# Latent rows turned by VectorE and DMA instead of TensorE in a two-layer hybrid trunk

## The chip, the core and the metric

The kernel runs on one core of a Trainium2 chip. The metric is the device time of one execution in microseconds; the median of three runs of the kernel before is 1133.07 us (1133.02 to 1134.05).

## The reference

A backbone of two layers with 256 latent tokens and 256 context tokens, width 2048, in float32. Each layer makes one wide input projection (5120 columns), three branches (a gated position-mixing MLP, windowed attention that also reads the context, Fourier mixing), gates them, concatenates them and projects back. Only the latents are returned, after the second layer.

```python
h = rmsnorm(x, g_pre[l]) * (1.0 + scale[:, None]) + shift[:, None]
h_c = rmsnorm(ctx, g_pre[l]) * (1.0 + scale_c) + shift_c
proj = h @ w_in[l]
...
y = mixer_branches(proj, latent_attn, g_sgu[l], w_sgu[l], b_sgu[l], w_fourier[l], b_fourier[l])
y = rmsnorm(y @ w_out[l], g_post[l])
x_new = x + gate[:, None] * y
```

The last line is where the change lies: in the second layer it adds x1, the latents that the first layer returned, to the gated and normalised projection.

## The kernel before

**Layout.** Nearly everything is held transposed: features on the 128 partitions, tokens along the free dimension. The tile `yo[k]` (k from 0 to 15) holds features 128k to 128k+127 of both streams, latents in columns 0 to 255 (`LAT`), context in 256 to 511 (`CTX`). After the first layer `yo[k][:, LAT]` holds x1, transposed. The output, however, has rows of tokens: the last projection (phase out1, function `finish`) takes 128 tokens at a time as the stationary operand and so makes its result with tokens on the partitions. Before the sum, x1 has to be turned to rows of tokens, in eight tiles of 128 tokens by 512 features: `x1[j, t]` for four groups of features j and two blocks of tokens t.

**Matmuls.** Float32 precision is had from two parts, a high and a low one: each weight tile of 128x1024 is loaded into one of three `raw` buffers (L433), cast to `whi` by ScalarE (ACT, L456), and the rest `wlo` is made by VectorE (DVE, L458). Products take three matmuls (`mm3`, L488 to L490) or two (`mm2`, L604 and L605). The function `fetch` keeps the split three tiles ahead of TensorE (PE); there are four buffers for each part.

**Order.** PE's instructions run in the order in which the program is written. Those of DVE, ACT, SP (SyncE, which issues the loads) and POOL are put in order by a scheduler, before the run; each engine then runs its list in that order, and an instruction that waits holds up all those behind it. Side work is written as generators and handed to a small planner (`Later`): each has a due time in a model clock that advances with the main matmuls (`later.tick`), runs to its next `yield` when it is due, and gives the delay to its next step there. `later.flush()` runs what is left.

**Layer 1 in order of time.** First units av and au (742 to 774 us), then fourteen units of one or two streams: au, cx (Fourier), ag and cg (gates), to 864 us; a flush; then k (to 886) and v (to 909) of both streams, eight q units with the attention heads as side work, eight bg units, and the last projection from 1029.5 us on. Side work between 778 and 868 us is the second half of branch A (`ps_mix`), the Fourier steps (`ps_f`, `ps_z`), and `boundary_ctx`: the context's new residual (`yo[k][:, CTX]`, DVE at L1279, then a DMA by POOL at L1280 that adds the old context to it), the sum of its squares (ACT L1284, DVE L1286, PE `ps_rs` L526) and its normalised form for k and v (L566, L570, L575).

**The gate of layer 1** (`mod_gate1`, L287 to L291) is a product of a vector with w_mod on DVE: 32 loads of 512 KB into two buffers `mraw`, two instructions of DVE for each, spread by `pace` over the phases k1, v1, q1, bg1 and out1 at low priority. Its four results lie in `ctrh`, `ctrl`, `nstrh` and `nstrl`; `gate1` finishes them (L302 to L309).

**The turn before** is the generator `turn` in `finish` (L1138 to L1149): four transposes by PE into a PSUM bank and one ACT copy to SBUF for each `x1[j, t]`, one every `YT` = 3.0 of the model clock. The tiles it writes are vv, mg, mgl, kt0 and kt1, which attention used before; `vv` is also the buffer of the Fourier weights early in the layer, and of the values of attention from the v units on. `close` reads the x1 tiles at the end.

Of the kernel before, what the change touches and what calls it, by code (L numbers as in the profile page):

```python
# [7 lines left out]
F32 = mybir.dt.float32  # L8
# [5 lines left out]
P = 128  # L14
D = 2048
KT = D // P
S = 256
# [49 lines left out]
def trunk_kernel(ctx: ExitStack, tc: tile.TileContext, xT, xhalf, cT, wss, wsl, wmod, win, wout0, wout1, const, vec, rows,  # L67
                 wmat, bs, sink, out):
    nc = tc.nc
    V, A, G, PE, DMA = nc.vector, nc.scalar, nc.gpsimd, nc.tensor, nc.sync  # L70

    pool = ctx.enter_context(tc.tile_pool(name="sb", bufs=1))
    psum = ctx.enter_context(tc.tile_pool(name="ps", bufs=1, space=bass.MemoryType.PSUM))
    W2K = 7
    cnt = [0]

    def sb(shape, dt, tag, bufs=1):
        cnt[0] += 1
        return pool.tile(shape, dt, tag=tag, bufs=bufs, name=f"{tag}_{cnt[0]}")

    def w2k(shape, dt=F32):
        return sb(shape, dt, "w2k", W2K)

# [4 lines left out]
    def ms_ps(name="ms"):  # L88
        cnt[0] += 1
        return psum.tile([P, 512], F32, tag="ms", bufs=2, name=f"ps_{name}_{cnt[0]}")  # L90


    yo = [sb([P, T], F32, f"yo{k}") for k in range(KT)]
# [42 lines left out]
    ident = identr.bitcast(F32)  # L136
# [195 lines left out]
    BYDVE = {10: 7, 15: 7}  # L332
    RING = "ctrl nstrl kt1 ws bsb hh11 hl11 ctrl yo8 nstrl kt1 ws bsb yo9 yo10 yo11".split()
    LOWC = 60
    YT = 3.0
    GATES = {2: 0, 14: 1}, {14: 2}, {12: 3}, {}
    YG = 6.5
    WARM = 4
# [38 lines left out]
    later = Later()  # L377
# [109 lines left out]
    def mm3(ps, st, mv, start, stop):  # L487
        PE.matmul(ps, st[0], mv[0], start=start, stop=False)  # L488
        PE.matmul(ps, st[0], mv[1], start=False, stop=False)  # L489
        PE.matmul(ps, st[1], mv[0], start=False, stop=stop)  # L490
# [13 lines left out]
    def split_into(hi, lo, src):  # L504
        A.copy(hi, src)  # L505
        V.tensor_tensor(out=lo, in0=src, in1=hi.bitcast(F32), op=ALU.subtract)  # L506
        return hi, lo
# [79 lines left out]
    FULL, LAT, CTX = slice(0, T), slice(0, S), slice(S, T)  # L587
    PASS = 0.648 / T

    def tunit(n, sl=None):  # L590

        sl = slice(0, n) if sl is None else sl
        ps = mm_ps("t")
        for k in range(KT):
            if k % 8 == 0:
                w = W.next()
            c = slice((k % 8) * P, (k % 8 + 1) * P)
            mm3(ps[:, sl], part(w, c), (hh[k][:, sl], hl[k][:, sl]), k == 0, k == KT - 1)
            later.tick(PASS * n)
        return ps  # L600
# [13 lines left out]
    def tunit1(streams):  # L614

        pss = [mm_ps("t") for _ in streams]
        for k in range(KT):
            if k % 8 == 0:
                w = W.next()
            for s, ps in zip(streams, pss):  # L620
                mm2(ps, part(w, slice((k % 8) * P, (k % 8 + 1) * P)), (hh, hl)[s][k], k)
                later.tick(PASS * S)
        return [joined(ps) for ps in pss]
# [12 lines left out]
    def layer(l):  # L636
        last = l == 1
# [241 lines left out]
        def fourier_mats():  # L879
            for j in range(2):  # L880
                ps = ms_ps("mg")
                mm3(ps, csp[j], wfp, True, True)
                split_into(mg[0][:, :, j], mg[1][:, :, j], ps.rearrange("p (g d) -> p g d", d=P))
            yield 0.0
# [47 lines left out]
        kt, vv = [], None  # L932
# [80 lines left out]
            later.add(turn_mask(), 7.0)  # L1013
        later.add(branch_a())
        later.add(fourier_mats(), 3.0)
        later.tick(0.0)
        state["phase"] = f"au{l}"
        for h in range(len(au), 4):
            ps = tunit1([0])[0] if last else tunit(n)
# [3 lines left out]
        for g in range(4):  # L1023
            ps = tunit1([0])[0] if last else tunit(n)
# [3 lines left out]
        for h in range(4):  # L1028
            ps = tunit1([0])[0] if last else tunit(n)
            gate(h, ps)  # L1030
        state["phase"] = f"cg{l}"
        for g in range(4):
            ps = tunit1([0])[0] if last else tunit(n)
# [11 lines left out]
        vv = sb([P, 1024], F32R, "vv"), sb([P, 1024], F32R, "mg")  # L1045
# [12 lines left out]
        for h in range(8):  # L1058
            ps = tunit1([0])[0] if last else tunit(n)
# [3 lines left out]
        for h in range(8):  # L1063
            ps = tunit1([0])[0] if last else tunit(n)
# [35 lines left out]
    def out_proj():  # L1100
# [30 lines left out]
        later.flush()  # L1131
        return acc

    def finish():

        x1 = {}

        def turn():  # L1138

            for j, tag in enumerate(("vv", "mg", "mgl", "kt0 kt1")):  # L1140
                tag = tag.split()
                tl = [sb([P, 2 // len(tag), 512], F32, t) for t in tag]
                for t in range(2):
                    x1[j, t] = tl[0][:, t] if len(tl) == 1 else tl[t][:, 0]
                    ps = ms_ps("x1")
                    for i in range(4):
                        PE.transpose(ps[:, i * P:(i + 1) * P], yo[4 * j + i][:, t * P:(t + 1) * P], ident)
                    A.copy(x1[j, t], ps)
                    yield YT  # L1149

        later.add(turn(), YT)
        state["phase"] = "out1"
        state["ones"] = sb([P, P], F32R, "join", 2)
# [161 lines left out]
    with tc.manual_schedule(engines={EN.PE}):  # L1315
# [12 lines left out]
        for k in range(KT):  # L1328
            q = w2k([P, T])
# [14 lines left out]
        ps = ms_ps("rs")  # L1344
# [16 lines left out]
        make_h(0, 0, rb0, [0, 1], e)  # L1361
        list(e)
        layer(0)
        state["acc"] = out_proj()
        layer(1)
        finish()


# [75 lines left out]
```

## Time and profile before

| | us |
|---|---|
| median of three runs | 1133.07 |
| profiled execution | 1132.31 |
| its span | 1130.5 |
| PE busy | 1122.0 |
| DVE busy | 927.6 |
| ACT busy | 528.5 |
| POOL busy | 33.7 |

The span is the time from the first to the last instruction of the profiled execution. Busy times of PE overlap with its weight loads (PEld). A row of the profile gives an engine, the line of the kernel, the operation, and the tile written and the tiles read; in a row of the timeline the first two numbers are the start and the length in us, and the bracket at its end is the idle time of that engine just before, with what ended it. "SPq" is SP's queue, where a DMA is issued; the DMA share is the mean busy share of the 16 DMA engines.

### The profile page before, as it was taken

Reading aid. Unit: us, or ns where it says so; the run is one execution under the profiler, and the core shown is the slowest. Engines: PE = TensorE matmul, PEld = TensorE weight load, DVE = VectorE, ACT = ScalarE, POOL = GpSimd, SP = SyncE. Lnnn points to the kernel's source line nnn. Section 1 sums busy time; section 2 is a strip of 40 time slices with the busy share of each in tenths; the row PEclk is TensorE's granted clock in tenths of the full one; section 3 lists DMA queues with packets and bytes.
Section 4 is the critical chain, followed back from the end, with each engine's and each line's share of the span. In section 5 each row is a group of like instructions: output and inputs, shape, how many; then the busy total and the mean of one; then the engine's idle time right before and its main releaser. Section 6 shows DMA issues by size and latency. Waiting matters only on the chain.

```text
span 1130.5 us, 16656 instructions
## 1 busy us (share of the span) xinstructions
PE 1122.0 (99%) x6117; PEld 921.5 (82%) x6117; DVE 927.6 (82%) x1649; ACT 528.5 (47%) x991; POOL 33.7 (3%) x41
## 2 busy tenths in 40 slices
PE   8999999999999999999999999999999999999998
PEld 3666788888888888888888888988888888888886
DVE  1578799989888788898999988397889789878883
ACT  5322433322235666642533334256665369857551
POOL 0000000000000000000000000030500000000000
PEclk9999999999999999999999999999999999999999
DMA  9999656566656344356556665276956686556972
GB/s 350 403 402 400 243 181 202 170 206 192 215 175 188 107 140 131 122 180 211 186 170 223 221 212 179 94 170 213 226 168 197 214 295 195 158 170 198 315 251 75
DMA packets 75250, 235.85 MB, mean 209 GB/s; under 512 B 8736, under 2 KB 13216, under 8 KB 75168
## 3 DMA queue, kind: packets, MB, share of 16 engines
q1 hardware_dynamic: 70992, 230.85, 61.4%
q0 software_dynamic: 4032, 3.67, 2.2%
q8 instruction: 48, 0.79, 0.3%
q14 instruction: 34, 0.28, 0.1%
q10 hardware_dynamic: 144, 0.26, 0.1%
HBM read 232.65 MB, written 2.10 MB: 208 GB/s over the span
## 4 chain that ended last, share of the span: by engine, by line
PE 96%; DVE 1%; ACT 1%; DMA 0%; issue 0%; SPq 0%; POOLq 0%; DVEq 0%; ACTq 0%
PE ps_t L488 15%; PE ps_t L490 15%; PE ps_t L489 15%; PE ps_t L604 10%; PE ps_t L605 5%; PE ps_v L1053 3%; PE ps_y L488 3%; PE ps_y L490 3%; PE ps_y L489 3%; PE ps_mod L181 2%; PE ps_av L488 2%; PE ps_av L489 2%; PE ps_av L490 2%; PE ps_tp L995 1%; PE ps_v L1054 1%; PE ps_au L488 1%
## 5 line engine op out<-in xcount | busy, mean ns | idle before, releaser
L456 ACT CAST whi<-raw 128x1024 fp32r<-128x1024 f32 (+1 forms) x209 | 216.4, 1037 | 320.6 <-PE ps_t L489 221.9
L488 PE MATMUL ps_t<-hh,whi 128*128 128x512 f32 (+1 forms) x752 | 290.6, 386 | 0.0
L490 PE MATMUL ps_t<-hh,wlo 128*128 128x512 f32 (+1 forms) x752 | 289.7, 385 | 0.0
L489 PE MATMUL ps_t<-hl,whi 128*128 128x512 f32 (+1 forms) x752 | 289.6, 385 | 0.0
L458 DVE TENSOR_TENSOR wlo<-raw,whi 128x1024 fp32r<-128x1024 f32 (+1 forms) x209 | 250.9, 1203 | 45.8 <-ACT whi L456 40.0
L253 DVE SCALAR_TENSOR_TENSOR macc<-mraw,cs,macc 128x512 f32<-128x512 f32 x360 | 250.0, 745 | 11.5 <-DMA mraw<-in_wmod_dram 11.2
L604 PE MATMUL ps_t<-hh,whi 128*128 128x512 f32 x512 | 184.9, 399 | 0.0
L490 PEld LDWEIGHTS ps_t<-hh,wlo 128*128 128x128 f32 x752 | 141.3, 188 | 28.5
L488 PEld LDWEIGHTS ps_t<-hh,whi 128*128 128x128 f32 x752 | 141.3, 188 | 26.9
L489 PEld LDWEIGHTS ps_t<-hl,whi 128*128 128x128 f32 x752 | 141.3, 188 | 26.4
L605 PE MATMUL ps_t<-hh,wlo 128*128 128x256 f32 x512 | 143.4, 280 | 0.0
L604 PEld LDWEIGHTS ps_t<-hh,whi 128*128 128x128 f32 x512 | 96.2, 188 | 21.5
L605 PEld LDWEIGHTS ps_t<-hh,wlo 128*128 128x128 f32 x512 | 96.6, 189 | 0.4
L570 ACT ACTIVATE hh<-w2k,sh 128x256 fp32r<-128x256 f32 x48 | 22.1, 503 | 72.7 <-DVE w2k L566 72.7
L488 PE MATMUL ps_y<-whi,hh 128*128 128x512 f32 x104 | 41.3, 397 | 0.0
L490 PE MATMUL ps_y<-whi,hh 128*128 128x512 f32 x104 | 40.6, 390 | 0.0
L489 PE MATMUL ps_y<-wlo,hh 128*128 128x512 f32 x104 | 40.5, 389 | 0.0
L488 PE MATMUL ps_av<-whi,hh 128*128 128x512 f32 x94 | 39.0, 415 | 0.6 <-ACT hh L570 0.6
L489 PE MATMUL ps_av<-wlo,hh 128*128 128x512 f32 x94 | 37.1, 395 | 0.0
L505 ACT CAST w2k<-ps_tp 128x512 fp32r<-128x512 f32 x40 | 23.4, 586 | 20.3 <-PE ps_scc L489 8.6
L518 POOL TENSOR_TENSOR rs_b<-rs_a,mhalf 128x2 f32<-128x2 f32 (+1 forms) x6 | 6.6, 1096 | 776.8 <-DVE mx L1245 584.8
L506 DVE TENSOR_TENSOR w2k<-ps_tp,w2k 128x512 fp32r<-128x512 f32 x40 | 27.4, 684 | 1.3 <-ACT w2k L505 0.5
(458 smaller groups left out, 1777.0 us busy)
## 6 DMA issues: line engine op xcount, KB each, us to landing
raw<-in_win_dram SPq DMA_DIRECT2D x160, 512.0 KB, 4.1
mraw<-in_wmod_dram SPq DMA_DIRECT2D x128, 512.0 KB, 4.2
raw<-in_wout_dram SPq DMA_DIRECT2D x60, 512.0 KB, 4.4
mraw<-in_wsl_dram SPq DMA_DIRECT2D x14, 512.0 KB, 7.2
yo<-in_xT_dram SPq DMA_DIRECT2D x16, 256.0 KB, 5.3
yo<-in_wsl_dram SPq DMA_DIRECT2D x16, 256.0 KB, 7.2
macc<-in_wsl_dram SPq DMA_DIRECT2D x7, 512.0 KB, 7.7
vv<-in_wsl_dram SPq DMA_DIRECT2D x7, 512.0 KB, 8.4
```

Of the source, the lines that this page charges most:

```text
L181: PE.matmul(self.ps[32 * kk:32 * kk + 32, 0:self.N], cpad[:, kg * 4 + kk], self.w[kg * 4 + kk], start=kg == 0, stop=kg == 3, tile_position ...
L253: V.scalar_tensor_tensor(out=acc[:, s], in0=w[:, kk % 2], scalar=c, in1=acc[:, s], op0=ALU.mult, op1=ALU.add)
L456: A.copy(ph, rc)
L458: self.last = V.tensor_tensor(out=pl, in0=rc, in1=ph.bitcast(F32), op=ALU.subtract)
L488: PE.matmul(ps, st[0], mv[0], start=start, stop=False)
L489: PE.matmul(ps, st[0], mv[1], start=False, stop=False)
L490: PE.matmul(ps, st[1], mv[0], start=False, stop=stop)
L505: A.copy(hi, src)
L506: V.tensor_tensor(out=lo, in0=src, in1=hi.bitcast(F32), op=ALU.subtract)
L604: PE.matmul(ps, w[0], h, start=k == 0, stop=False)
L605: PE.matmul(ps[:, 0:S], w[1], h[:, 0:S], start=False, stop=k == KT - 1)
L1053: PE.matmul(vps[t], hi, wk, start=k == 0, stop=False)
```

## The change

x1 is now turned during layer 1 by a new generator, `x1_rows`, which is started in the second layer beside branch A and the Fourier weights, with a delay of 7.0 and a step every `YS` = 6.0 of the model clock. It takes the buffer `vv` for four pieces of 128x256. Step k turns `yo[k][:, LAT]` with VectorE's transpose, which works in squares of 32x32: within each square rows and columns are exchanged, and the squares stay where they are. Two steps later four DMAs, one for each band of 32 partitions, put the squares in their places in a scratch tile in DRAM, `x1d[g]`, of 256 tokens by 512 features; each moves 32 x 8 runs of 32 floats. That is 16 transposes and 64 DMAs on SP's queue. In `finish`, `turn` loads each `x1[j, t]` (128 tokens by 512 features, 256 KB) from the scratch with one DMA, in place of the four PE transposes and the ACT copy. `YT` is 6.0 instead of 3.0.

```diff
+    dram = ctx.enter_context(tc.tile_pool(name="dram", bufs=1, space=bass.MemoryType.DRAM))
...
-    YT = 3.0
+    YT, YS = 6.0, 6.0
...
         later.add(fourier_mats(), 3.0)
+        if last:
+            later.add(x1_rows(), 7.0)
...
+    x1d = {}
+
+    def x1_rows():
+        v = sb([P, 4, S], F32, "vv")
+        ts = [v[:, i] for i in range(4)]
+        for k in range(KT + 2):
+            if k >= 2:
+                g, i = divmod(k - 2, 4)
+                if i == 0:
+                    x1d[g] = dram.tile([S, 512], F32, tag=f"x1_{g}", name=f"x1_{g}")
+                for q in range(4):
+                    f = i * P + 32 * q
+                    DMA.dma_start(x1d[g][:, f:f + 32].rearrange("(b t) f -> t b f", t=32),
+                                  ts[i][32 * q:32 * q + 32].rearrange("p (b f) -> p b f", f=32))
+            if k < KT:
+                V.transpose(ts[k % 4], yo[k][:, LAT])
+                yield YS
...
-                    ps = ms_ps("x1")
-                    for i in range(4):
-                        PE.transpose(ps[:, i * P:(i + 1) * P], yo[4 * j + i][:, t * P:(t + 1) * P], ident)
-                    A.copy(x1[j, t], ps)
+                    DMA.dma_start(x1[j, t], x1d[j][t * P:(t + 1) * P])
                     yield YT
```

## The prediction

> **What bounds the kernel now.** I read the page first (busy shares, then the chain that ended last), and after it the busy time by stretch for layer 1 and the last projection.
>
> ```profile
> span 1130.5 us, 16656 instructions
> PE 1122.0 (99%) x6117; PEld 921.5 (82%) x6117; DVE 927.6 (82%) x1649; ACT 528.5 (47%) x991; POOL 33.7 (3%) x41
> PE 96%; DVE 1%; ACT 1%; DMA 0%; issue 0%; SPq 0%; POOLq 0%; DVEq 0%; ACTq 0%
> ...
> 780.00:830.00 50.00, 50.00 (x314) 44.77 (x313) 42.03 (x89) 30.45 (x68) 16.23 (x18) 1.00 0.79 209
> 830.00:864.00 34.00, 34.00 (x198) 29.64 (x197) 31.39 (x59) 21.78 (x39) 1.12 (x1) 1.00 0.56 173
> 864.00:886.00 22.00, 22.00 (x127) 19.03 (x125) 17.00 (x32) 8.48 (x18) 0.00 (x0) 1.00 0.64 204
> 1033.00:1068.00 35.00, 35.00 (x171) 28.99 (x170) 30.78 (x42) 21.17 (x31) 0.00 (x0) 1.00 0.81 269
> ```
>
> TensorE (PE) is the bound: 96% of the chain, and in the stretches where the change acts (780 to 886 the new work, 1033 to 1068 the old transposes) it has no idle time at all. The columns after it are PEld, VectorE (DVE), ACT, POOL, the clock and the DMA share. So an instruction taken from PE counts in full, and added work counts only where something that PE waits for in its fixed order comes late. DVE has 16 us left over the 106 us of the first three stretches.
>
> **What is removed.** The 32 transposes at L1147 and the 8 copies at L1148.
>
> ```profile
> 1033.43 0.39 PE L490 MATMUL ps_y<-whi,hh 128*128 128x512 f32 x1
> 1033.66 0.60 PE L1147 MATMUL ps_x<-identr,yo 128*128 128x128 f32 x4
> 1034.02 0.47 PE L488 MATMUL ps_y<-whi,hh 128*128 128x512 f32 x1
> 1034.33 0.39 PE L489 MATMUL ps_y<-wlo,hh 128*128 128x512 f32 x1
> ...
> L1147 PE MATMUL ps_x<-identr,yo x32: 270/272/273, 1033.7 to 1066.8; 128*128 128x128 f32 x32
> ```
>
> Starts are what counts, since matmuls overlap. A group of four takes 1034.02 - 1033.66 = 0.36 us, and the product behind it 0.31 instead of the usual 0.23 (1033.43 to 1033.66), so 0.44 us a group and 8 x 0.44 = **3.5 us** off PE. The 8 copies go from ACT, which is 21.17 of 35 us busy there: nothing. DVE had 30.78 us of work in these 35 us, and PE now leaves it 31.5; weight tiles are split three ahead, and the next stretch is lighter, so I take **+0.3** for it (0 to 1.0).
>
> **Added: 16 VectorE transposes**, 128x256 from SBUF.
>
> ```profile
> L259 DVE STREAM_TRANSPOSE mraw<-macc 128x512 f32<-128x512 f32 x24 | 16.2, 693 | 0.0
> 793.54 2.09 DVE L1279 TENSOR_TENSOR yo<-yo,rbs 128x256 f32<-128x256 f32 x6
> ...
> 809.26 1.23 DVE L458 TENSOR_TENSOR wlo<-raw,whi 128x1024 fp32r<-128x1024 f32 x1 [0.28 <-ACT whi L456]
> 816.54 1.23 DVE L458 TENSOR_TENSOR wlo<-raw,whi 128x1024 fp32r<-128x1024 f32 x1 [0.42 <-ACT whi L456]
> 823.24 1.23 DVE L458 TENSOR_TENSOR wlo<-raw,whi 128x1024 fp32r<-128x1024 f32 x1 [0.42 <-ACT whi L456]
> 827.39 0.40 DVE L1286 TENSOR_TENSOR acc<-acc,w2k 128x256 f32<-128x256 f32 x1
> 828.62 0.58 PE L526 MATMUL ps_rs<-ones,acc 128*128 128x1 f32 x4
> ```
>
> Half of 693 ns, and the step of a like-sized add (2.09/6), both give 0.35 us: 5.6 us in all. In the built order, five stand before 793, where DVE waits, five from 808 to 828, the rest later. The five take 1.75 us, the three waits there give back 1.12, so the context's sum of squares is ready 0.6 us later than 827.8, and PE reads it at 828.62: **0** (0 to 0.3). The others stand beside light work. A transpose also waits for the four stores that read its buffer four steps ago; in the built order they stand at least a whole weight tile ahead of it, and I take nothing for them (a late store would show as DVE waiting for a DMA).
>
> **Added: 64 stores** of 32 KB, each 256 pieces of 128 B, 16 per DMA engine, on SP's queue. Only the kernel's first load (ct, 128 rows of 128 B) shows pieces of this size, and it is a read; the context's accumulating DMAs (1 KB pieces) are the dearest kind in the trace.
>
> ```profile
> GB/s 0 0 0 0 0 0 0 0 0 0 0 0 0 0 0 0 0 0 0 0 0 0 0 0 0 0 0 0 0 0 0 0 0 0 0 46 67 74 72 31
> q1 hardware_dynamic: 126, 0.01, 4.7%
> ...
> 796.00:816.00 20.00, 20.00 (x124) 17.83 (x124) 18.19 (x43) 11.89 (x30) 12.47 (x15) 1.00 1.09 253
> q0 software_dynamic: 2283, 2.08, 69.4%
> ...
> 808.17 1.05 ACT L456 CAST whi<-raw 128x1024 fp32r<-128x1024 f32 x1 [1.14 <-DMA raw<-in_win_dram]
> 810.40 0.27 DVE L506 TENSOR_TENSOR w2k<-ps_f,w2k 1x128 fp32r<-1x128 f32 x1
> 811.01 0.28 PE L488 MATMUL ps_z<-ctrh,w2k 128*128 128x256 f32 x1
> ```
>
> In the first 2 us, 4.7% of 16 engines over 126 pieces is 12 ns each; at the peak of 74 GB/s a piece takes 16 x 128 B / 74 GB/s = 28 ns with its gap. The accumulating piece is 0.694 x 16 x 20 / 2283 = 97 ns. I take 12 to 28 ns (0.2 to 0.45 us a store): nearest in size and kind; 97 ns is a rival. Stores stand two or three behind each weight load. From 796 to 816 the DMA share is over 1, and ACT waited for a weight tile at 808.17. Behind that cast on ACT stands the cast of a row whose split on DVE (810.67 done) PE reads at 811.01: 0.34 us of slack. Two stores stand ahead of that tile, 0.4 to 0.9 us, so **+0.3** (0.05 to 0.55).
>
> **Moved: the queue of SP and the gate's products.** This is the dearest term. All tasks are flushed at the end of the cg1 units, so the last 16 stores stand in a row on SP. Behind them, in the built order, the loads of w_mod (mraw) for L289/L291 come later: the third load stood in SP's queue at 868.43, and now stands behind the weight load that went out at 879.75.
>
> ```profile
> 868.43 0.33 SPq L287 DMA_DIRECT2D mraw<-in_wmod_dram  x1
> ...
> 879.75 0.33 SPq L433 DMA_DIRECT2D raw<-in_win_dram  x1
> ...
> 890.90 0.74 DVE L291 SCALAR_TENSOR_TENSOR ctrh<-mraw,cs,ctrh 128x512 f32<-128x512 f32 x1
> 897.86 1.54 DVE L291 SCALAR_TENSOR_TENSOR ctrh<-mraw,cs,ctrh 128x512 f32<-128x512 f32 x2 [2.64 <-DMA mraw<-in_wmod_dram]
> 908.63 0.82 DVE L611 TENSOR_TENSOR join<-join,ps_v 128x256 f32<-128x256 f32 x2 [2.27 <-ACT join L610]
> ...
> 915.90 1.22 DVE L458 TENSOR_TENSOR wlo<-raw,whi 128x1024 fp32r<-128x1024 f32 x1 [0.63 <-ACT whi L456]
> 920.25 1.23 DVE L458 TENSOR_TENSOR wlo<-raw,whi 128x1024 fp32r<-128x1024 f32 x1 [0.19 <-ACT whi L456]
> 921.39 0.42 DVE L506 TENSOR_TENSOR w2k<-mgl,w2k 128x256 fp32r<-128x256 f32 x1
> 921.86 0.19 PEld L490 LDWEIGHTS ps_sc<-kt,w2k 128*128 128x128 f32 x1 [0.23 <-DVE w2k L506]
> ...
> mraw<-in_wmod_dram SPq DMA_DIRECT2D x5, 512.0 KB, 4.7
> mraw<-in_wmod_dram SPq DMA_DIRECT2D x128, 512.0 KB, 4.2
> ...
> L287 SPq DMA_DIRECT2D mraw<-in_wmod_dram x32: 327/328/426, 729.9 to 1082.0; - x32
> DMA to landing us min/median/max: 3.3/5.0/6.9
> ```
>
> The same ten tiles of products still stand ahead of the joins of v (L611 at 908.63), and DVE runs in order. There are two mraw buffers, so a load waits for the products that free one. The third tile's second product stays behind k's rope, and is done by 891.3 (the row at 890.90 and what follows it). Then three loads follow one another in that buffer, each landing in l us: the first two are multiplied in 1.6 us each, and behind the third stand its products, 0.4 us until the other buffer's tile lands, and that tile's (3.4 in all). So L611 starts at 891.4 + 3 l + 2 x 1.6 + 3.4 = 898.0 + 3 l, where it was 908.63. From 880 to 900 a load took 4.7 us, two often going out together; they will now be spread, and the median of all 128 is 4.2, so I take 4.4: L611 at 911.2, 2.6 us late. DVE then waits only 0.63 + 0.19 us until the first rope of q, whose low half PE already awaits (0.23 us, last column of 921.86). So PE stalls about 2.6 - 0.8 = **+1.8 us**. At 3.3 us it is nothing; at 5.9 (rival B's row) it is 7.1 - 0.8 = 6.3.
>
> The 8 loads of x1 go out behind waits that other loads had anyway (same tiles' last readers), into buffers read only in the last products: nothing, unless those are late. SP has time for the issues, at 0.33 us each.
>
> **Sum:** -3.5 + 0.3 + 0 + 0.3 + 1.8 = -1.1 us. The profiled execution took 1132.31 us (span 1130.5 and 1.8 around it), and would take 1131.2; the median of the runs is 1133.07, so I forecast **1132.0 us**. Its own bounds: -3.5 - 0.2 (the wait at 921.86) gives 1129.4; 0.3 + 0.55 + 6.3 + 1.0 - 3.5 = +4.65 gives 1137.7.
>
> **Rivals.** (A) The full gain: the products catch up before L611, because loads land in under 3.6 us once SP sends them singly. 1133.07 - 3.5 = 1129.6. For it: 2.27 us of slack at L611; against it: five loads at 4.7.
> (B) Slower by the same chain:
>
> ```profile
> mraw<-in_wmod_dram SPq DMA_DIRECT2D x2, 512.0 KB, 5.9
> ```
>
> from 900 to 910 a load took 5.9 us. At that l, L611 is at 915.7, 7.1 late, PE stalls 6.3: 1133.07 - 3.5 + 0.6 + 6.3 = 1136.5. It decides from l = 5.0 on (stall 3.6, no net gain), and passes +2.3 from about 5.7. Against it: the last-tile loads that crowded 900 to 910 (half-tile hl loads) are now spread.
> (C) A 128 B write costs what an accumulating piece does. At 97 ns a store holds every engine 1.55 us; 48 stores in the 84 us from 780 to 864 are 74 us, and the free share there, 1 - 0.70, is 25: weights come up to 49 us late, 1179 at the worst; at half that price (0.78 us, 37 us of work) 12 us, 1142. [...] No row of this trace shows such a write to DRAM.
>
> **Numbers.** The forecast's mechanism 0.45, A 0.18, B 0.27, C 0.10. A measurement here tells about 0.2%, 2.3 us. Faster by more: A and 0.10 of the forecast, 0.28. Within: 0.30 of the forecast and 0.02 of B, 0.32. Slower: the rest, 0.40. The range 1129.2 to 1139.5 takes in A, the forecast's own bounds (1129.4 to 1137.7) and the way from there to C's lower price, 1142; it leaves out C and the far ends of the rest, less than 2 in 10.
>
> **What would show it.** No ps_x rows, and PE in the last projection 3.5 us shorter; stream transposes of 0.35 us; packets of 128 B at 12 to 28 ns; L611 on the first v tiles 2 to 3.5 us later relative to PE, and PE waiting for DVE at the first ps_sc. I am wrong if PE stands still anywhere between 780 and 864 for over 1 us (C, or the transposes), or if L611 is on time (A).

## The result and the profile after

The changed kernel took 1137.63 us (median of 6 runs, 1136.54 to 1141.0), the kernel before 1133.37 beside it (1132.86 to 1134.53): ratio 1.004, 95% interval 1.0025 to 1.0054. It is **4.3 us slower**, where 1.1 us less was forecast (1132.0; range 1129.2 to 1139.5). The profiled execution of after took 1138.22 us. Its page:

```profile
span 1136.4 us, 16688 instructions
...
PE 1120.1 (99%) x6085; PEld 918.7 (81%) x6085; DVE 931.6 (82%) x1665; ACT 523.5 (46%) x983; POOL 33.7 (3%) x41
...
PE 88%; DVE 4%; DMA 4%; issue 2%; ACT 1%; POOL 0%; SPq 0%; POOLq 0%; DVEq 0%; ACTq 0%
```

PE executes 32 instructions less and is still 99% busy, but its share of the chain of waits went from 96 to 88%: DVE and DMA now stand in it with 4% each. So the path to the end leaves PE in some places. The row of the last projection's main product, before and after (first and last start), shows that the removed work is gone:

```profile
L488 PE MATMUL ps_y<-whi,hh x104: 389/389/474, 1029.5 to 1110.8; 128*128 128x512 f32 x104
```

```profile
L489 PE MATMUL ps_y<-whi,hh x104: 388/389/403, 1038.8 to 1116.4; 128*128 128x512 f32 x104
```

From first to last it takes 77.6 us instead of 81.3, **3.7 us less** (3.5 forecast). But it starts 9.3 us later. The view of what PE waited for tells where that came from (engine, tile and line, what was awaited, us in total, times, longest):

```profile
PE ps_sc L489 <- ACT w2k L506: 3.4, 1, 3.4
...
PE ps_av L490 <- DVE wlo L459: 1.8, 1, 1.8
PE ps_f L491 <- DVE w2k L507: 1.3, 1, 1.3
...
PE ps_rs L527 <- DVE acc L1306: 0.6, 1, 0.6
...
PE ps_f L489 <- ACT w2k L506: 0.4, 1, 0.4
```

The wait at ps_av is near 762 us, ahead of the first transpose (781.3) and the first store (781.8). It took 0.2 to 1.8 us in most of the profiles below: 0.2 in the one without any store (e1), 1.0 in one whose transposes begin only at 923.8 (e10), and nothing in two of those with stores. So I take it for a matter of the single execution and not of the change. In what follows "late" means later than in before, less the lateness of the row of ps_t products that begins at 774.2 us in before (776.2 in the changed kernel, so 2.0). Two places remain.

**From 780 to 864 us.** The stretches of the prediction's table, after:

```profile
780.00:830.00 50.00, 47.99 (x292) 42.20 (x290) 41.64 (x89) 28.71 (x63) 15.92 (x18) 1.00 0.88 215
830.00:864.00 34.00, 33.44 (x200) 29.31 (x199) 31.43 (x63) 21.24 (x38) 1.57 (x1) 1.00 0.74 187
```

PE was at 50.00 and 34.00 in these and now stands still for 2.6 us of them. DVE was busy for 0.4 us *less* in the first one (42.03 before) though it had ten transposes more to do: it stood. Its order of time there (start, length, then in brackets the idle time ahead and what ended it), and after it the group of all 16 transposes, and that of the stores from 800 to 830:

```profile
811.30 0.43 DVE L1154 STREAM_TRANSPOSE vv<-yo 128x256 f32<-128x256 f32 x1
...
811.97 0.42 DVE L1154 STREAM_TRANSPOSE vv<-yo 128x256 f32<-128x256 f32 x1
...
813.95 0.41 DVE L1306 TENSOR_TENSOR acc<-acc,w2k 128x256 f32<-128x256 f32 x1
817.71 0.45 DVE L1154 STREAM_TRANSPOSE vv<-yo 128x256 f32<-128x256 f32 x1 [3.36 <-DMA x<-vv]
```

```profile
L1154 DVE STREAM_TRANSPOSE vv<-yo x16: 396/433/446, 781.3 to 872.6; 128x256 f32<-128x256 f32 x16
...
L1151 SPq DMA_DIRECT2D x<-vv x17: 303/460/1193, 799.8 to 827.9; - x17
...
DMA to landing us min/median/max: 2.6/6.2/8.6
```

A transpose is 0.43 us (0.35 forecast) and harmless. But two went out within 0.7 us, and the third, the eighth in all, found its buffer still being read: the last of the four stores that read it had left SP at 809.0 and landed 8.6 us later. The median of the stores issued here is 6.2 us. DVE, in order, stood 3.36 us with the context's sums and the splits for ps_f behind it, and PE waited for these at 819 to 821.

**At the first scores.** SP's queue, the gate's products on DVE, and PE:

```profile
869.63 8.12 SPq L1151 DMA_DIRECT2D x<-vv  x16
877.86 7.31 SPq L434 DMA_DIRECT2D raw<-in_win_dram  x3
885.22 0.43 SPq L288 DMA_DIRECT2D mraw<-in_wmod_dram  x1
```

```profile
889.75 0.75 DVE L292 SCALAR_TENSOR_TENSOR ctrh<-mraw,cs,ctrh 128x512 f32<-128x512 f32 x1 [1.93 <-DMA mraw<-in_wmod_dram]
...
917.53 0.75 DVE L612 TENSOR_TENSOR join<-join,ps_v 128x256 f32<-128x256 f32 x2
```

```profile
929.27 0.64 PE L489 MATMUL ps_sc<-kt,w2k 128*128 128x512 f32 x1 [3.44 <-ACT w2k L506]
```

The 16 flushed stores keep SP for 8.1 us, three weight loads follow, the last of which waits for its buffer and leaves at 884.8 (the load at 879.75 in the prediction's rows), and the gate load that stood at 868.43 goes out at 885.22. DVE's product that frees the gate load's buffer was done at 875.6, so it is SP's order that held it. The joins of v come at 917.53 instead of 908.63; PE reached v 4.5 to 4.8 us later, so they are 4.4 us late against it (2.6 forecast), and PE stands 3.44 us (1.8 forecast). What came behind had not been forecast at all; the clock is the third column from the right:

```profile
926.00:928.00 2.00, 0.00 (x0) 0.00 (x0) 1.95 (x5) 1.78 (x5) 0.00 (x0) 1.00 0.78 236
928.00:930.00 2.00, 0.73 (x2) 0.33 (x2) 1.78 (x3) 1.60 (x3) 0.00 (x0) 0.87 0.91 285
930.00:932.00 2.00, 1.81 (x5) 1.19 (x5) 1.78 (x4) 0.93 (x2) 0.00 (x0) 0.50 1.08 369
932.00:934.00 2.00, 2.00 (x10) 1.68 (x9) 1.63 (x6) 1.61 (x4) 0.00 (x0) 0.78 0.87 305
```

After the stall TensorE was granted half its clock for some 2 us, and 0.78 to 0.87 of it around them: 0.26 + 1.0 + 0.44 = 1.7 us of clock lost over these rows, most of it while PE had work.

### The profile page after: what moved, and what is told of

It reads as the page before. It is cut to its first block, busy times and chain, and to the rows that moved or that the text cites. A ratio compares the mean times of both kernels' runs of the same rounds, so it can differ in the third digit from the quotient of the medians.

```text
span 1136.4 us, 16688 instructions
## 1 busy us (share of the span) xinstructions
PE 1120.1 (99%) x6085; PEld 918.7 (81%) x6085; DVE 931.6 (82%) x1665; ACT 523.5 (46%) x983; POOL 33.7 (3%) x41
## 4 chain that ended last, share of the span: by engine, by line
PE 88%; DVE 4%; DMA 4%; issue 2%; ACT 1%; POOL 0%; SPq 0%; POOLq 0%; DVEq 0%; ACTq 0%
PE ps_t L489 15%; PE ps_t L491 15%; PE ps_t L490 15%; PE ps_t L605 8%; PE ps_t L606 4%; PE ps_y L491 3%; PE ps_y L489 3%; PE ps_y L490 3%; PE ps_mod L182 2%; PE ps_av L489 2%; PE ps_av L490 2%; PE ps_av L491 2%; PE ps_tp L996 1%; PE ps_v L1056 1%; DMA mraw<-in_wmod_dram 1%
## 5 line engine op out<-in xcount | busy, mean ns | idle before, releaser
L254 DVE SCALAR_TENSOR_TENSOR macc<-mraw,cs,macc 128x512 f32<-128x512 f32 x360 | 249.8, 745 | 12.3 <-DMA mraw<-in_wmod_dram 12.2
```

The costliest lines, as they stand in the source:

```text
L254: V.scalar_tensor_tensor(out=acc[:, s], in0=w[:, kk % 2], scalar=c, in1=acc[:, s], op0=ALU.mult, op1=ALU.add)
```

## The experiments

Times are medians; "against before" is the difference to the median of the kernel before, run beside it on the same chip (1132.75 us for e1 to e4, 1133.67 for e5 to e8, 1133.9 for e9 to e12, 1133.95 for e13 and e14).

| kernel | us | against before | 95% interval of the ratio |
|---|---|---|---|
| changed | 1137.63 | +4.3 | 1.0025 to 1.0054 |
| e1 no stores | 1129.12 | -3.6 | 0.9958 to 0.9981 |
| e2 last four held, spaced | 1130.89 | -1.9 | 0.9975 to 0.9993 |
| e3 stores by GpSimd | 1139.28 | +6.5 | 1.0038 to 1.0065 |
| e4 pieces of 1 KB | 1131.38 | -1.4 | 0.9976 to 0.9996 |
| e5 last four held, 4 buffers | 1134.71 | +1.0 | 1.0005 to 1.0025 |
| e6 last four held, 16 buffers | 1130.64 | -3.0 | 0.9967 to 0.9986 |
| e7 flush only | 1131.72 | -1.95 | 0.9976 to 0.9994 |
| e8 spread | 1131.72 | -1.95 | 0.9975 to 0.9993 |
| e9 16 buffers, flush | 1140.4 | +6.5 | 1.0047 to 1.0074 |
| e10 all late | 1146.08 | +12.2 | 1.0096 to 1.0123 |
| e11 changed again | 1138.15 | +4.3 | 1.0034 to 1.006 |
| e12 16 buffers, step 3.5 | 1141.59 | +7.7 | 1.0054 to 1.0079 |
| e13 gate loads by GpSimd | 1139.05 | +5.1 | 1.0031 to 1.0056 |
| e14 e13 with 16 buffers | 1146.73 | +12.8 | 1.0096 to 1.0132 |

### e1: without the stores

```diff
-                for q in range(4):
...
-                    DMA.dma_start(x1d[g][:, f:f + 32]...)
...
-                    DMA.dma_start(x1[j, t], x1d[j][t * P:(t + 1) * P])
+                    DMA.dma_start(x1[j, t]..., xhalf[0, j][:, 2 * t:2 * t + 2])
```

> The 16 VectorE transposes stay, the 64 stores are left out, and the tiles of x1 are loaded from the input's own layout (256 KB each, the same bytes as before in 8 loads), so the output is not the reference's. Theory 1 (the stores in SP's queue make the gate's w_mod loads late, and TensorE stands still at the first scores) and theory 2 (the stores load the DMA engines from 796 to 826 us, so that rows and context sums come late) both expect the removed TensorE transposes alone to be left: 1133.4 - 3.5 = 1129.9 us (1129 to 1131), joins of v (L612 of the kernel after) within 1 us of before relative to PE, no PE wait over 1 us at ps_sc, ps_f, ps_rs. Rival 3 (the transposes on VectorE or the loads of x1 are what costs): 1134 or more.

It took 1129.12 us, 3.6 under before. PE's waits from 780 us to the end:

```profile
PE ps_x L1209 <- ACT w2k L1201: 0.5, 1, 0.5
PE ps_sc L491 <- DVE w2k L507: 0.4, 1, 0.4
```

Both theories held and the rival fell: 16 transposes on DVE and 8 loads of the size of x1's cost nothing that shows, and the whole of the 7.9 us between this and the changed kernel comes with the stores.

### e2: the last four steps behind v

Here the 16 stores that were flushed go out in q, and each of the 12 transposes ahead stands behind a weight split.

```diff
-            later.add(x1_rows(), 7.0)
+            later.add(x1_rows(0, 12), 7.0)
...
+            if last and h == 2:
+                later.add(x1_rows(12, KT), 2.0)
...
-                V.transpose(ts[k % 4], yo[k][:, LAT])
+                with tc.issue_after(W.last.ins):
+                    V.transpose(ts[k], yo[k][:, LAT])
```

> The first 12 transposes and their 48 stores run as in the changed kernel; the last 4 with their 16 stores go behind v, among the units of q, through buffers that are free by then, so that at the end of cg1 nothing is flushed to SP ahead of the gate's loads. Theory 1: the stall of 3.4 us at the first ps_sc and the slow clock behind it (about 1.4 us) are gone: 1137.6 - 4.8 = 1132.8 us (1131.8 to 1134). Theory 2: the first 48 stores are what costs, so at most 1 us is won: 1136.6 or more, with PE still late at ps_f and ps_rs. If both hold, in between, with the two parts to be read off PE's start of ps_rs (about 830 us) and of ps_sc (about 922 us).

1130.89 us, better than either theory: the stall at ps_sc is gone, and there is none from 780 to 864 either, with 48 stores still there (PE at v 0.4 us late). That didn't fit theory 2 and pointed at the spacing of the transposes: no transpose here waits for a buffer.

### e3: stores by GpSimd; e4: pieces of 1 KB

```diff
-                    DMA.dma_start(x1d[g][:, f:f + 32]...,
+                    G.dma_start(x1d[g][:, f:f + 32]...,
```

> The same 64 stores at the same places in the program, but issued by GpSimd on its own queue; SP's queue has the order of the kernel before. Theory 1 alone (all is SP's order): 1130 to 1131 us, the gate's loads and the joins of v on time, no stall at ps_sc. Theory 2 (the stores cost by loading the engines, whoever issues them): no stall at ps_sc, but PE 2 to 3 us late at ps_rs, 1132 to 1133.5 us. Rival 4 (pieces of 128 B are dear wherever they go, and GpSimd's are dearer still): 1137 us or more.

1139.28 us, worse than changed; but not by rival 4's reason. SP's order was that of before and the first scores came without a stall, while DVE stood far longer for its buffers (idle time ahead of the transposes, us and times):

```profile
  DMA x<-vv: 10.1, 3
```

The stores wait on GpSimd's queue among the accumulating DMAs (ahead of stores GpSimd stood 1.7 us for these and 3.2 us for the transposes, and it took 0.58 us in the median to issue one, SP 0.45 in the changed kernel), so a buffer came free later. On the DMA engines they were no dearer: from 780 to 864 us GpSimd's queue took 27.7% of 16 engines, 16.7% before, which is 2.3 us of one engine for each of the 64 stores (an estimate, which puts all of the difference down to them); at the 19 ns a piece that are read below it would be at most 4.9 us on SP's queue.

In e4 each store writes 1 KB pieces:

```diff
-                    DMA.dma_start(x1d[g][:, f:f + 32].rearrange("(b t) f -> t b f", t=32),
-                                  ts[i][32 * q:32 * q + 32].rearrange("p (b f) -> p b f", f=32))
+                    DMA.dma_start(x1d[g][f // 2:f // 2 + 16]..., ts[i][32 * q:32 * q + 32])
```

> The same number of stores and bytes, but each partition's 256 values are written as one piece of 1 KB instead of eight of 128 B, in another order, so the output is not the reference's; 8 times fewer packets. In the built order more of them go out before 864 us and none is flushed behind cg1. Theory 2 with the piece size as its cause: PE within 1 us of before at ps_rs, 1129.5 to 1131 us. Theory 2 with the mere number of transfers ahead of weight loads as its cause: still 2 to 3 us late at ps_rs, 1132 to 1133.5 us. Theory 1 expects no stall at ps_sc, since nothing stands in a row ahead of the gate's loads.

1131.38 us, between the two answers. DVE still waited 2.0 us for buffers, PE stood 1.4 us from 780 to 864, and with nothing flushed there was no stall at the scores. So small pieces alone are not what the changed kernel loses by: the wait for buffers stays with large ones. It is shorter, though: 2.0 us in all and 1.1 at the longest, against 3.5 and 3.3 in e5 below, which has the four buffers and no flush either. And e4 lies 2.4 us lower than e5 by their differences to before, so the pieces have a part in how late a buffer comes free. The price of a piece can be read in the changed kernel from 869 to 878 us, where SP issued little but the stores (packets of the window, then of the queue: packets, MB, share of 16 engines):

```profile
DMA packets 4213, 1.11 MB, mean 123 GB/s; under 512 B 4061, under 2 KB 4061, under 8 KB 4213
...
q1 hardware_dynamic: 4213, 1.11, 55.7%
...
x<-vv SPq DMA_DIRECT2D x16, 32.0 KB, 1.8
```

0.557 x 16 x 9 us over 4213 packets is 19 ns each, the larger ones included: inside the 12 to 28 ns forecast, far from 97. If the 152 larger packets went at the 20 GB/s of an engine in before (14.16 MB in 52.5% of 16 engines over the 84 us from 780 to 864), the small ones took about 12 ns each, some 10 GB/s (an estimate).

### e5 and e6: the buffers alone

Both hold the last four steps back behind v as in e2, but leave the 12 ahead as the changed kernel has them. e5 keeps its four buffers, e6 has 16, with the stores within a place or two of e5's.

```diff
 e6 against e5
-            ts = [v[:, k % 4] for k in range(KT)]
+            ts = [v[:, 0]] + [yo[k][:, LAT] for k in range(KT - 1)]
```

> The first 12 transposes and 48 stores stand exactly where the changed kernel has them, with its four buffers; only the last 4 with their 16 stores go behind v, so the gate's loads stand in SP's queue as before the change. (In the run with the last four held, the 12 had also been set behind weight splits on VectorE, and no transpose there waited for a buffer.) Theory B (what is lost from 780 to 864 us is VectorE standing 3.4 us for the stores that read its buffer): PE reaches v (886.5 us before) about 2.8 us late, DVE waits 2 to 3.5 us for x<-vv, no stall over 0.5 at ps_sc, and the time is about 0.8 us under before (-3.6 + 2.8), 1131.5 to 1133 us. Theory D (the loss there was the DMA load, or a matter of that execution): as with the last four held, 0.7 us late at v, about 2.5 us under before, 1130 to 1131 us.

> As the run with four buffers, but the transposed tiles go into 16 buffers: each into the latent half that the transpose before it has read, so no transpose waits for a store. Same stores at the same places. Theory B: no DVE wait for x<-, PE at v at most 0.8 us late, 2.5 to 3.3 us under before: 1129.7 to 1130.7 us, and 1.5 to 2.5 us under the run with four buffers. Theory D: as the run with four buffers, within 0.7 us.

1134.71 and 1130.64 us: **4.1 us** between them, on the same chip, with intervals that lie apart. Theory B held, and its size came out larger. DVE's wait in e5, PE's from 780 to 930 us in e5, then in e6:

```profile
DVE vv L1159 <- DMA x<-vv: 3.5, 2, 3.3
```

```profile
PE ps_f L491 <- DVE w2k L507: 1.3, 1, 1.3
PE ps_f L489 <- ACT w2k L506: 0.7, 1, 0.7
PE ps_f L489 <- DVE w2k L865: 0.2, 1, 0.2
```

```profile
PE ps_rs L527 <- DVE acc L1314: 0.2, 1, 0.2
```

From 780 to 930 PE stood only 2.2 us in e5, but it was 3.6 us late at v (e6 not at all): the clock fell here too, behind waits of 1.3 us at most (the columns are those of the windows above).

```profile
820.00:822.00 2.00, 1.41 (x6) 1.32 (x7) 1.90 (x6) 1.19 (x4) 0.00 (x0) 0.68 0.44 59
822.00:824.00 2.00, 2.00 (x8) 1.71 (x7) 2.00 (x5) 1.91 (x9) 0.00 (x0) 0.50 0.85 250
```

The mean granted clock of whole executions says the same: 0.996 to 1.0 over the 11 of e5 (the longest, 1138.91 us, at 0.996), 0.998 to 1.0 over the 10 of e6. The profiled execution of e5, which at 1136.36 us lies above its median, has 1.4 us more of a wait in the last projection (ps_y for wlo), which e6 and the changed kernel don't have; it stands in four other profiles too (1.1 to 2.2 us), and no run here tells its cause.

### e7: the flush alone

```diff
+        yield 60.0
-        for k in range(KT + 2):
-            if k >= 2:
+        for k in range(12, KT + 2):
+            if k >= 14:
...
+              with tc.issue_after(W.last.ins):
                 V.transpose(ts[k % 4], yo[k][:, LAT])
```

(The first three quarters of x1 are loaded from the input's layout, as in e1.)

> Only the last 4 transposes and their 16 stores are made, and flushed at the end of cg1 as in the changed kernel; the first 12 tiles aren't stored, and their three quarters of x1 are loaded from the input's layout, so the output is not the reference's. Theory 1 (the flush alone makes the gate's loads late): nothing late at v, then a PE wait of 2.5 to 3.5 us at the first ps_sc for ACT's copy, a granted clock under 0.8 in the 2 us behind it, together 4 to 5 us: 1133 - 3.6 + 4.6 = 1134 us (1133 to 1135). Rival (it needs the lateness of 780 to 864 as well): under 1131 us.

1131.72 us: 1.7 us above e1 by their differences to before (their intervals just overlap), but not by the stall I expected. With PE 0.4 us later at v than in before, instead of 4.8, the flush began 5 us earlier:

```profile
864.26 6.15 SPq L1152 DMA_DIRECT2D x<-vv  x12
870.51 1.84 SPq L434 DMA_DIRECT2D raw<-in_win_dram  x3
872.41 0.42 SPq L288 DMA_DIRECT2D mraw<-in_wmod_dram  x1
```

The gate load went out at 872.41 (868.43 before, 885.22 changed), the joins of v came at 909.77 (908.63 before), and PE did not wait at the first scores (921.9); its two waits for scores, 0.4 us each, came at 936.9 and 938.0 (before has the second of them, too). So the flush is dear only with the gate's load pushed far enough back. How far is set in SP's list, before the run: counting the weight loads that leave SP from 740 us to this gate load, there are 42 in before, 43 in e7 and 44 in the changed kernel. It is the 44th that waits for its buffer; in e7 it left at 880.49, behind the gate load. What makes up e7's 1.7 us isn't shown: against e1 its one profile loses 0.7 us between the first scores and the last projection, 0.4 of it in the wait at 936.9, and 0.7 us in the last projection, 0.5 of it in a wait.

### e8: the stores spread

```diff
-    YT, YS = 6.0, 6.0
+    YT, YS = 6.0, 9.0
...
-            later.flush()
+            later.flush(rows_gen)
...
-        ts = [v[:, i] for i in range(4)]
+        ts = [v[:, 0]] + [yo[k][:, LAT] for k in range(KT - 1)]
```

(`flush` leaves out the task that it is given; each transpose stands behind a weight split as in e2.)

> A version of the change: 16 buffers as above, each transpose set behind a weight split on VectorE, one step per about 9 us of the planner's clock instead of 6, and the task is left out of the flush at the end of cg1, so that the stores run on singly through k, v, q and the gates. Theories 1 and B together: no PE wait over 0.5 us at ps_sc or ps_f, 2.5 to 3.6 us under before: 1129.3 to 1130.5 us. Rival (the sum of stores and gate loads is too much for SP or the DMA engines wherever they stand): 1132 us or more, with weight tiles late in q.

1131.72 us, 1.95 under before; from 780 to 1020 us PE waited 0.4 us in all. The theories held in the trace; the gain is 0.5 us short of the least that they gave.

### e9, e10 and e11: mended in part, all late, and the change once more

e9 is the changed kernel with e6's line for ts alone; e10 makes all 16 steps from the second unit of q on, through four context halves.

```diff
 e9
-        ts = [v[:, i] for i in range(4)]
+        ts = [v[:, 0]] + [yo[k][:, LAT] for k in range(KT - 1)]
...
 e10
-    YT, YS = 6.0, 6.0
+    YT, YS = 6.0, 4.0
...
-            later.add(x1_rows(), 7.0)
...
+            if last and h == 1:
+                later.add(x1_rows(), 0.0)
...
-                V.transpose(ts[k % 4], yo[k][:, LAT])
+                with tc.issue_after(W.last.ins):
+                    V.transpose(yo[k % 4][:, CTX], yo[k][:, LAT])
```

> The changed kernel with one thing mended: the transposed tiles go into 16 buffers (each into the latent half that the transpose before it has read), all else as it is, the flush at the end of cg1 too. With no wait for a buffer more steps are ready early, and in the built order the first gate load of this stretch stands behind 37 weight loads (34 before the change, 36 in the changed kernel). Theory: the buffers' 4 us are won back and the flush's share is left: 1.7 us (as with the flush alone) to 2.8 us (changed kernel less the one with four buffers and no flush) above the run with 16 buffers and no flush: 1132 to 1133.5 us against 1133.4 before; no DVE wait for x<-. Rival (the flush does no harm once TensorE isn't late already): 1130.2 to 1131 us.

> Another version: all 16 transposes and 64 stores go behind v, from the second unit of q on, set behind weight splits on VectorE, through four context halves that are free by then; SP's queue is as before the change until 926 us, and the stretch of the context's sums is left alone. Theory: 2.6 to 3.6 us under before, 1129.8 to 1130.8 us. Rival (VectorE, 28.6 of 30 us busy from 930 to 960, or SP, can't take them there, or the loads of x1, which now wait for the last stores, come late): 1132 us or more, with PE waits in q or at the last products.

> The changed kernel once more, beside these. If the wait for buffers and the flush are both causes: 3.5 to 5 us above before as it was, 2 to 3.5 us above the run with four buffers and no flush (by their ratios to before), 4 to 6 us above the one with 16 buffers and the flush; in the trace again a DVE wait of 2 us or more for x<-vv ahead of PE's late ps_f, and a PE wait of 1 us or more at the first ps_sc. What comes out otherwise belongs to that one execution.

e9 was a surprise: 1140.4 us, 2 us *worse* than changed by the medians (the two intervals overlap a little) though no transpose waited. SP's queue and the gate's products:

```profile
859.73 10.49 SPq L1151 DMA_DIRECT2D x<-yo  x18
870.32 19.32 SPq L434 DMA_DIRECT2D raw<-in_win_dram  x7
889.97 1.90 SPq L288 DMA_DIRECT2D mraw<-in_wmod_dram  x2
```

```profile
889.20 2.32 DVE L292 SCALAR_TENSOR_TENSOR ctrh<-mraw,cs,ctrh 128x512 f32<-128x512 f32 x3
```

```profile
PE ps_sc L489 <- ACT w2k L506: 5.4, 2, 4.2
```

Seven weight loads now stand between the flush and the gate's load (45 by the count of e7), and in the built order DVE's first gate products stand behind k's rope as well. The gate load goes out 21.5 us later than before; the stall at the scores grew to 5.4 us. When it went out, the last of the weight loads had just left, and the product that frees its own buffer was done at 889.95. So the place in SP's list and DVE's own order can't be told apart here; e14 does that. e10 fell by its rival's last clause, for a reason of the same kind: in the last projection the gate's loads stood behind loads of x1 that wait for the last stores, and PE stood for the last gate row:

```profile
PE ps_gate L308 <- ACT w2k L506: 10.2, 1, 10.2
```

e11 repeated the changed kernel's readings: 4.3 above before, 4.0 us of DVE waits for x<-vv, 2.4 us at the first ps_sc. The third comparison of its expectation failed with e9.

### e12: 16 buffers and a shorter step

```diff
-    YT, YS = 6.0, 6.0
+    YT, YS = 6.0, 3.5
...
+        ts = [v[:, 0]] + [yo[k][:, LAT] for k in range(KT - 1)]
```

> The changed kernel with 16 buffers and the planner's step for the turning tasks cut from 6.0 to 3.5, so that all 64 stores are out before cg1 ends and nothing is left to flush; in the built order the first gate load of this stretch stands behind 34 weight loads, as before the change (37 with 16 buffers and a step of 6.0, which took 10 us more than the run without stores). Theory: the place of the gate loads in SP's queue is what the flush costs, so that loss is gone, and with no wait for a buffer only the load on the DMA engines is left: 2 to 3.4 us under before, no PE wait over 1 us from 780 to 930 us. Rival (64 stores in the 84 us from 780 to 864, four behind nearly each weight load, are too many for the stretch with a DMA share near 1): 0 to 3 us above before, PE late at ps_f and ps_rs with ACT waiting for raw.

1141.59 us: the rival was nearer. PE was 3.9 us late at ps_rs, with ACT waiting 3.1 us for raw at 812.6, and the larger part was lost behind it, where PE waited for weight tiles from 858 to 890 us and ACT again for their load:

```profile
PE ps_t L606 <- DVE wlo L459: 3.2, 4, 1.1
PE ps_t L605 <- ACT whi L457: 2.4, 1, 2.4
```

```profile
879.73 1.05 ACT L457 CAST whi<-raw 128x1024 fp32r<-128x1024 f32 x1 [3.03 <-DMA raw<-in_win_dram]
```

So the gate's place in SP's queue (42 by the count of e7, as in before) and free buffers aren't enough. Ahead of 830 us four stores behind nearly each weight load go with late weights, as the rival has it; for the larger loss behind 858 this is not shown, since the last store had left SP by 863.6, and SP's weight loads then waited mostly for buffers that DVE frees (14.0 us for wlo).

### e13 and e14: the gate's loads off SP's queue

```diff
-                    DMA.dma_start(w, wmod[12 + c, kk // 4][:, kk % 4:kk % 4 + 2])
+                    G.dma_start(w, wmod[12 + c, kk // 4][:, kk % 4:kk % 4 + 2])
```

> The changed kernel, with the gate's w_mod loads (L288) issued by GpSimd on its own queue, where nothing is waited for between 836 us and the end; the stores, their flush and the weight loads stay on SP as they are, and so do the four buffers. If the flush costs by standing ahead of the gate loads: no DVE wait over 1 us for mraw from 885 to 920, joins of v on time relative to PE, no stall over 0.5 us at the first ps_sc, and 2.5 to 3.2 us under the changed kernel: 1.3 to 2.5 us above before, 1134.8 to 1136.3 us. If it costs by what stands on SP behind it (weight loads) or by its load on the DMA engines: within 1 us of the changed kernel, 1137 to 1139 us.

> As that, with the 16 buffers: the run with 16 buffers and the flush (1140.4 us, 6.6 above before) with its gate loads taken off SP. If the waits for buffers and the late gate loads are the whole loss: 2 to 3.3 us under before, 1130.5 to 1132 us, like the run with 16 buffers and no flush. If late weight loads behind the flush carry part of it: 1134 us or more, with PE waiting for whi or wlo between 860 and 930 us.

The place came out as expected in e13, the time not: the joins of v (916.52) no longer waited for gate products, and from 864 to 1020 us this was all that PE waited for:

```profile
PE ps_sc L491 <- DVE w2k L507: 0.4, 1, 0.4
```

But in the profile the clock fell behind nearly the same waits at ps_f (0.56 and 0.59 from 820 to 828 us, PE 5.8 us late at v instead of 2.8). That isn't this execution alone: the mean granted clock was 0.996 or 0.997 in all five, 0.999 or 1.0 in before beside it. And PE waited in the last projection:

```profile
PE ps_y L490 <- DVE wlo L459: 2.2, 2, 1.7
PE ps_gate L308 <- DVE w2k L507: 0.7, 1, 0.7
```

DVE's own waits for the gate's rows there are no longer than in the changed kernel (7.0 us for nstrl in both), so the loads by GpSimd aren't shown to be the cause. So it took 1139.05 us, as in the second answer of its expectation: the lateness of the gate loads is shown to come from their place in SP's queue, but no time was won by mending it. e14 had neither cause as I had named them and was the slowest beside e10, 1146.73: PE stood 6.2 us at ps_sc. The gate's loads waited there for DVE itself, whose products stood late in its own order, as in e9; the first one left at 887.01, 3.0 us ahead of e9's, with PE 3.3 us ahead of e9's at v, so taking SP out of the way won them nothing:

```profile
885.96 2.32 DVE L292 SCALAR_TENSOR_TENSOR ctrh<-mraw,cs,ctrh 128x512 f32<-128x512 f32 x3
```

## Why the prediction was wrong

The steps e1, e6, e5 and changed (e11) make a ladder, each the one before with one thing more. It closes by construction; what it gives is the size of each rung, in differences to before. Only e5 and e6 ran on the same chip. Each difference is known to 1 to 1.5 us by its interval, so the rungs of 4.1 and 3.2 us are clear of the noise and that of 0.6 is not.

| step of the prediction | forecast | measured |
|---|---|---|
| TensorE transposes off PE, DVE in the last projection | -3.5 + 0.3 | -3.6 (e1) |
| stores ahead of weight loads | +0.3 | +0.6 (e6 - e1) |
| a transpose waits for its buffer's stores | 0 | **+4.1** (e5 - e6) |
| the flush ahead of the gate's loads | +1.8 | +3.2 (e11 - e5) |
| sum | -1.1 (with the rest 0) | +4.3 |

- **The step that failed** is the one sentence on the buffers: "in the built order they stand at least a whole weight tile ahead of it, and I take nothing for them (a late store would show as DVE waiting for a DMA)". It showed just so, 3.36 us. The weight tiles there are some 3.3 us apart (loads left SP at 804.26 and 807.52); a store took 6.2 us to land in the median, the awaited one 8.6, where the DMA share was 1.13 (800 to 820 us). The order was as the sentence says; what it left out is the landing. The prediction had a share of 1.09 in a quoted row and used it for the weight loads' sake, not for the stores' own landing. It had no end of the range for this wait, so it is luck that the measured 1137.6 us lies within 1129.2 to 1139.5: that room had been left for the flush and for rival C.
- **The flush** was the right mechanism, with its place, its first victim (the joins of v) and the stall at the first ps_sc, and mis-sized: the joins were 4.4 us late, not 2.6, the stall 3.4, not 1.8, and the slow clock behind it was not in the sum. By the prediction's formula 4.4 us late is a landing of l = 5.0 us for each gate load, the point from which its rival B decides. The three loads of that chain landed after 4.7, 4.0 and 5.1 us, which is 0.6 of the missing 1.8 us over three times 4.4; the rest is a start 0.6 us later and smaller gaps. (B's "passes +2.3 from about 5.7" leaves out B's own 0.6 us; with them it is 5.5.) Alone the flush costs 1.7 us (e7), and not by the stall. What it costs hangs on where the built order puts the gate's loads and products, which changed from kernel to kernel: mending the buffers alone moved them further back and won nothing (e9). So the ladder's last rung would have another size in another order.
- **Right:** the 3.5 us, that DVE's work costs nothing (0.43 us a transpose, not 0.35), the price of a piece (19 ns or less), the loads of x1. Rival C fell. "I am wrong if PE stands still anywhere between 780 and 864 for over 1 us" is what happened (1.27 us in one wait, 2.6 in all), by a way that was named under neither of its two heads: not the pieces, not the transposes, but the buffer between them.
- **Open:** why the weights come late from 858 us in e12, why the scheduler's built order puts DVE's gate products behind k's rope in e9 and e14, what e7 loses, and why e13 won nothing with its stall gone. None of these was tried.

**A version that beats both** is e6: 16 buffers, each but the first the half that the transpose before it has read, 12 steps as they were and four behind v. It is 3.0 us under before (ratio 0.9977, interval 0.9967 to 0.9986), 0.6 us short of the change with its stores for nothing (e1).

## What to carry to other kernels

A ring of buffers that a DMA reads has to cover the DMA's landing under the load of its own stretch (here 6.2 us in the median and 8.6 for the awaited store), not only its issue (0.45 us); with four buffers instead of 16 that cost 4.1 us (e5, e6). Put "landing in that stretch over the shortest spacing of the writers" beside the number of buffers before taking a wait for zero. A flush of many small DMAs on an ordered queue can cost what stands behind it in that queue (here 16 stores kept SP for 8.1 us, and the gate's load went out 16.8 us later than before); the place of those loads is worth counting in weight loads from the built order, and so is the place of the instructions that free their buffers (with the gate's loads off SP's queue, PE still stood 6.2 us in e14). A stall of a bound TensorE can be dearer than its length (here 3.4 us and 1.7 us of clock), where the clock falls behind it (0.50 from 930 to 932).

## What was not expected of the hardware

- Half the clock came behind one wait of 3.44 us (0.50 from 930 to 932), behind one of 2.4 us in e11 (0.50 from 930 to 932 there, too), and behind 0.7 and 1.3 us within 3 us in e5 (0.50 from 822 to 824); behind 1.1 and 1.3 us in e13 it was 0.56 from 820 to 824 and 0.59 from 824 to 828. Waits of 0.4 and 1.3 us at the same place in the changed kernel, and of 1.0 and 1.3 in e11, left it at 1.00. So the length of the waits alone doesn't tell here whether the clock falls; what does, no run shows.
- A store took SP 0.45 us to issue in the median, up to 1.56, where a weight load takes 0.33, and it landed after 1.8 us in the median from 869 to 878 us and 6.2 from 800 to 830.
